# Attention units of a hybrid diffusion trunk put into a fixed TensorE order

## The chip, the cores and the metric

The kernel runs on one core of one Trainium2 chip. The metric is the device time of one execution in microseconds (us). Everything is float32; matmuls marked fp32r take operands that were split into a high part and a remainder, so most products are three matmuls.

## The reference, cut to what matters

One layer of a trunk: 512 latent and 128 context tokens (640 together), width 1024. One input projection feeds four mixers; each mixer's output goes through a branch matrix to width 1024, is multiplied by a sigmoid gate of its own, and the four are summed; an output projection and an MLP follow. Three of the mixers are attention with 8 heads: windowed (`sq`, `sk`, `sv`, with a sink logit), grouped-query (`gq`, ...) and multi-head latent attention (`mla_*`).

```python
def _joint_attention(q, segments, scale, sink=None):
    ...
        s = jnp.einsum(spec, q, k).astype(jnp.float32) * scale
    ...
    m = jnp.max(s, axis=-1, keepdims=True)
    e = jnp.exp(s - m)
    den = jnp.sum(e, axis=-1, keepdims=True)
    p = e / den
    ...
        o = jnp.einsum(spec, p[..., off:off + n_k].astype(v.dtype), v)
```

A latent query block of 128 tokens reads 640 keys (context and latent); in the windowed mixer it reads 384 or 512. The context query block reads 128 keys.

## The kernel before, in words

Activations lie transposed in SBUF as `hT` (channels on partitions, 640 tokens). The attention work is cut into **units**: a unit (`unit`, L800) is one query block `qt` (0 to 3 latent, 4 context) of a pair of heads. It does the scores on TensorE into PSUM, the negated row maximum on DVE (L818 or L835), the exponential with row sums on ACT (L819 or L840), the reciprocal on DVE (L821 or L847), the multiplication of the 128 x W weights `P` by it on POOL (L809), the transposes of `P` by TensorE (L856) with copies to `PT` on ACT and DVE (L858, L860), the products with the values (L1009 in the windowed and grouped-query mixers, L1185 in MLA), and the evacuation as a split pair (L506, L142).

- Where W is 640, the two heads are done one after the other: each has a PSUM tile `sc` of its own, two banks with 320 columns used in each. Two such tiles exist (pool `pss`, four banks). Otherwise both heads share one `sc` tile, a bank for each.
- `run_gqa` runs 20 units (two groups `j2` of 10) for the windowed mixer (n=1) and again for the grouped-query mixer (n=3). The queries of the second group are projected between the groups. Then `gates(n)` projects that branch's gates: 8 column groups (`gate_steps`), each of two halves of 24 matmuls of 320 columns (L365 to L367, into `mm`), a copy to `sig` by ACT (L694), and a sigmoid over 128 x 2560 after four groups (L697).
- `merge(n, ...)` multiplies a mixer's projected output by its gates (L365 to L367 with `oh`, `ol`, then L980, L981).
- `mla` projects queries and keys from low-rank latents. For each head pair `jj` it makes Q (`mQ`), rotary queries (transposes into `pj`, L1152), values (L1166) and keys (`mK`, `Kp`), and then five units; here a score is three matmuls (L949, L950, L1182). Beside them `side` holds 27 steps (L211 and what follows) of the next modulation rows, eight matmuls and a 512 KB load each, three steps after each unit. `ada_ps` is one bank of which two halves are used in turn.

Weights come by DMA on the queue of SyncE (`wr`, three buffers), are copied to `wh` by POOL (L139) and get their remainder `wl` from DVE (L142).

The order of instructions on each engine is made by the framework's scheduler when the program is built, from the program order and the dependencies; a block under `in_order(PE)` keeps the traced order on TensorE. Before the change, the attention stages are not under it. All 128-wide PSUM tiles come from eight banks: `sc` 4, `mm` 2 (in MLA `ada_ps` and `pj` instead), `tp`/`pv` 2.

Of the kernel before, what the change touches and what calls it, by code (L numbers as in the profile page):

```python
# [20 lines left out]
T = TS + TP  # L21
# [43 lines left out]
def trunk(ctx, tc, I, O):  # L65
# [26 lines left out]
    pss = ctx.enter_context(tc.tile_pool(name="pss", bufs=2, space=PSUM))  # L92
# [15 lines left out]
    def sc_tile():  # L108
        return pss.tile([128, 2, 512], F32, tag="sc", name="sc")
# [387 lines left out]


# [189 lines left out]
    def gate_steps(n, sig):  # L688
# [16 lines left out]
    with tc.tile_pool(name="hx", bufs=1) as hx:  # L705
# [25 lines left out]
        fill, due = dense(), 0.0  # L731

        def beside(share):

            nonlocal due
            due += share
            while due > 0:
                due -= next(fill, 100.0)

        with in_order(PE):  # L740
            for hp in range(2):
                lev = hgrn_levels(*qfk[hp], hx)
                while True:
                    try:
                        beside(next(lev))
                    except StopIteration as e:
                        A, QP = e.value
                        break
                for share in hgrn_out(hp, *qfk[hp], A, QP, hx):
                    beside(share)  # L750
            for _ in fill:
                pass
# [47 lines left out]
    def unit(n, c, heads, qt, nk, score, pv_mm, sink=False, bands=None):  # L800
# [11 lines left out]
        if W > 512:  # L812

            for i in range(2):
                sv = sc_tile()[:, :, 0:W // 2]
                for a in range(2):
                    score(sv[:, a], i, a * (W // 2), W // 2)
                V.tensor_reduce(out=negm[:, i:i + 1], in_=sv, axis=AX.XY, op=ALU.max, negate=True)  # L818
                S.activation(out=Pt[:, i, 0:W].rearrange("p (a n) -> p a n", a=2), in_=sv, func=AF.Exp,  # L819
                             bias=negm[:, i:i + 1], accum_out=den[:, i:i + 1])  # L820
                V.reciprocal(out=rden[:, i:i + 1], in_=den[:, i:i + 1])  # L821
                weigh(i)
        else:
            sv = sc_tile()[:, :, 0:W]
# [26 lines left out]
        for j, kt in enumerate(range(0, nk, 2)):  # L851
            kn = min(2, nk - kt)
            tp = tp_tile().rearrange("p (k i) t -> p k i t", i=2)
            for i in range(2):
                for kk in range(kn):
                    PE.transpose(out=tp[:, kk, i], in_=Pt[:, i, 128 * (kt + kk):128 * (kt + kk) + 128], identity=ident)  # L856
            if j % 2 == 0:
                S.activation(out=PT[:, kt:kt + kn], in_=tp[:, 0:kn], func=AF.Copy)  # L858
            else:
                V.tensor_copy(out=PT[:, kt:kt + kn], in_=tp[:, 0:kn])  # L860
        o = pv_tile()
        for kt in range(nk):
            for a in range(2):
                pv_mm(o[64 * a:64 * a + 64, 0:128], a, kt, PT[:, kt, a], kt == 0, kt == nk - 1)
        o_evac(n, c, 128 * qt, o[:, 0:128])

    def gqa_like(n, qn, kn, ck, cv, ok, ov_, norm):
# [38 lines left out]
        def queries(j2):  # L906
            QQ = big(F32R, 2, 2, T, name="Q")
            Q = [QQ[:, a] for a in range(2)]
            wq = wgroup(q_cols(OFF[qn], j2), 0, 256)
            bank = mm_tile if j2 else sc_bank  # L910
            ps = tok_block(wq, 256, hT, 0, bank())
            for tt in range(NT):
                x = prepare(tt, ps, 4, norm and norm[0], None)
                if tt + 1 < NT:
                    ps = tok_block(wq, 256, hT, tt + 1, bank())

                tp = (mp_tile if j2 else tp_tile)()
                for j in range(2):
                    PE.transpose(out=tp[:, j], in_=x[:, 128 * j:128 * j + 128], identity=ident)
                q_split(tp[:, 0:2], [x[:, :, 128 * tt:128 * tt + 128] for x in Q], 0.125)  # L920
            return Q
        return queries, K, Vt
# [67 lines left out]
    def run_gqa(n, queries, Q0, K, Vt, tiles, sink, bands):  # L990
        for j2 in range(2):
            Q = queries(j2) if j2 else Q0
            for qt, i in [(qt, i) for qt in range(5) for i in range(2)]:
                ks, j = tiles(qt), 2 * j2 + i

                def score(out, a, k0, kn):
                    Qa = Q[a][:, i, 128 * qt:128 * qt + 128]
                    done = 0
                    while done < kn:
                        first = ks[(k0 + done) // 128] * 128 + (k0 + done) % 128  # L1000
                        step = 128 - (k0 + done) % 128
                        while done + step < kn and ks[(k0 + done + step) // 128] * 128 == first + step:
                            step += 128
                        step = min(step, kn - done)
                        qk_mm(out[:, done:done + step], Qa, K_part(K, first, step), a)
                        done += step

                def pv_mm(out, a, kt, PTa, start, stop):
                    PE.matmul(out=out, lhsT=Vt[:, ks[kt], 64 * a:64 * a + 64], rhs=PTa, start=start, stop=stop)  # L1009
                unit(n, j, (j, 4 + j), qt, len(ks), score, pv_mm, sink=sink, bands=bands(qt))  # L1010

    queries, K, Vt = gqa_like(1, 'sq', 'sk', I['cache_swa_k'][0, 0], I['cache_swa_v'][0, 0], O['swa_k'], O['swa_v'], None)
# [4 lines left out]
    run_gqa(1, queries, Q0, K, Vt, swa_tiles, True, swa_bands)  # L1017
    sig = gates(1)
# [5 lines left out]
    queries, K, Vt = gqa_like(3, 'gq', 'gk', I['cache_gqa_k'][0, 0], I['cache_gqa_v'][0, 0], O['gqa_k'], O['gqa_v'],  # L1024
# [4 lines left out]
    run_gqa(3, queries, Q0, K, Vt, full_tiles, False, lambda qt: None)  # L1029
    sig3 = gates(3)  # L1030


    def mla():
# [96 lines left out]
        psm[1].close()  # L1130
        ex = ExitStack()
        psx = ex.enter_context(tc.tile_pool(name="psx", bufs=1, space=PSUM))
        ada_ps = psx.tile([128, 2, 256], F32, name="ada_ps")
        side.extend(ada_part(2, ada_ps[:, 0], modrow) + ada_part(3, ada_ps[:, 1]) + ada_part(4, ada_ps[:, 0]))

        def pj_tile():
            return psx.tile([128, 512], F32, tag="pj", name="pj")
# [3 lines left out]
        for jj in range(4):  # L1141
# [5 lines left out]
            t_block(wu['uq'][0], 128 * jj, cX, ev, bank=sc_bank)  # L1147
            for t4, tts in ((0, range(4)), (4, range(4, 5))):
                tp = pj_tile().rearrange("p (i t) -> p i t", t=128)
# [3 lines left out]
                for a in range(2):  # L1153
# [6 lines left out]
                    copy_r(to[64:128], f(to[0:64]))  # L1160
            if jj % 2 == 0:
                wv = [(x[0][:, 128 * jj:128 * jj + 256], x[1][:, 128 * jj:128 * jj + 256]) for x in wu['ukv'][1]]
                for kt in range(6):
                    ps = tok_block(wv, 256, kX, kt, pj_tile())
                    for i in range(2):
                        S.activation(out=Vs[jj + i][:, kt], in_=ps[:, 128 * i:128 * i + 128], func=AF.Copy)  # L1166
            Vt = Vs[jj]
            K = new_K("mK")

            def ev(ps, t0, tn):  # L1170
                for a, b in ((t0, min(t0 + tn, T)), (max(t0, T), t0 + tn)):
                    if a < b:
                        k_evac(ps[:, a - t0:b - t0], K, a, b - a)
            t_block(wu['ukv'][0], 128 * jj, kX, ev, halves=((0, 384), (384, 384)), bank=sc_bank)
            for qt in range(5):
                ks = full_tiles(qt)

                def score(out, a, k0, kn):
                    t = slice(128 * qt, 128 * qt + 128)
                    b = slice(ks[0] * 128 + k0, ks[0] * 128 + k0 + kn)  # L1180
                    qk_mm(out, Qa[a][:, t], K_part(K, b.start, kn), a, last=False)
                    PE.matmul(out=out, lhsT=QR[a][:, t], rhs=KRo[:, b], start=False, stop=True)  # L1182

                def pv_mm(out, a, kt, PTa, start, stop):
                    PE.matmul(out=out, lhsT=Vt[:, ks[kt], 64 * a:64 * a + 64], rhs=PTa, start=start, stop=stop)  # L1185
                unit(n, jj, (0, 1), qt, len(ks), score, pv_mm)
                side_steps(3)
# [155 lines left out]
```

## Time and profile before

| | us |
|---|---|
| median of 3 runs | 1501.13 (1498.35 to 1501.28) |
| profiled execution | 1502.2 |
| its span, first to last instruction | 1500.4 |
| mean granted TensorE clock | 0.991 of full |

The profiled execution is 1.1 us above the median, and 1.8 us lie around its span. In the timeline a row gives start and length in us, engine, line, operation, output and inputs; a matmul's length includes its way through the array, so the distance between two starts is what one costs when they follow each other. The stages are: windowed units 327 to 475, keys and queries of the grouped-query mixer and a merge 475 to 575, grouped-query units to 690, MLA's projections with a merge and gates to 795, MLA's head preparation and units to 945, the last merge to 975.

### The profile page before, as it was taken

How to read it: one execution, taken by the hardware profiler on the slowest of the kernel's cores; microseconds unless marked ns; L12 is line 12 of the kernel's file. 1: busy time of each engine (PE TensorE's matmuls, PEld its weight loads, DVE VectorE, ACT ScalarE, POOL GpSimd, SP SyncE). 2: the span in 40 equal slices, each digit the busy share in tenths (PEclk: the TensorE clock that was granted, in tenths of full speed). 3: DMA queues.
4: the chain of work that ended last, by engine and by line, in shares of the span. 5: the costliest groups of instructions: out<-in, count | busy, mean ns of one | idle time of the engine just before them, and what ended most of it. 6: DMA issues, size and time to landing. Idle time of an engine off the chain costs nothing.

```text
span 1500.4 us, 26709 instructions
## 1 busy us (share of the span) xinstructions
PE 1430.5 (95%) x10969; PEld 1302.2 (87%) x10969; DVE 796.1 (53%) x1447; ACT 481.4 (32%) x1161; POOL 432.2 (29%) x456
## 2 busy tenths in 40 slices
PE   6999999899999999999998998998999999999996
PEld 5898998899898998999996677988898998898995
DVE  4347657476643788433725566746243444444446
ACT  4334333333443235442124565225220110110112
POOL 2015325243321545222213334124111111112114
PEclk9999999999999999999999999999999999999998
DMA  9421212121112131112224601221343223222221
GB/s 328 128 85 58 70 49 64 50 68 50 45 43 59 34 84 37 33 42 74 80 68 143 224 15 43 99 85 56 112 129 101 80 71 98 71 70 71 75 66 70
DMA packets 138225, 121.17 MB, mean 81 GB/s; under 512 B 22296, under 2 KB 119412, under 8 KB 138104
## 3 DMA queue, kind: packets, MB, share of 16 engines
q1 hardware_dynamic: 138104, 119.47, 26.4%
q8 instruction: 86, 1.41, 0.4%
q14 instruction: 35, 0.29, 0.1%
HBM read 115.96 MB, written 3.49 MB: 80 GB/s over the span
## 4 chain that ended last, share of the span: by engine, by line
PE 70%; issue 13%; DVE 8%; POOL 5%; ACT 2%; DMA 1%; POOLq 0%; DVEq 0%; SPq 0%; ACTq 0%
PE mm L365 12%; PE mm L366 11%; PE mm L367 11%; PE mm L381 4%; PE mm L382 4%; PE mm L383 4%; PE tp L856 3%; POOL wh L139 3%; PE pv L1009 3%; PE sc L383 3%; PE sc L381 2%; PE sc L382 2%; PE sc L949 2%; PE sc L950 2%; DVE wl L142 1%
## 5 line engine op out<-in xcount | busy, mean ns | idle before, releaser
L139 POOL TENSOR_SCALAR wh<-wr 128x1024 fp32r<-128x1024 f32 (+3 forms) x136 | 156.7, 1154 | 536.4 <-PE mm L366 290.4
L142 DVE TENSOR_TENSOR wl<-wr,wh 128x1024 fp32r<-128x1024 f32 (+3 forms) x160 | 198.9, 1247 | 160.0 <-POOL wh L139 120.8
L365 PE MATMUL mm<-hTh,wh 128*128 128x320 f32 x704 | 220.5, 313 | 2.0 <-DVE qA L520 0.9
L367 PE MATMUL mm<-hTh,wl 128*128 128x320 f32 x704 | 219.2, 311 | 0.0
L366 PE MATMUL mm<-hTl,wh 128*128 128x320 f32 x704 | 218.2, 310 | 0.0
L366 PE MATMUL mm<-h2Tl,wh 128*128 128x320 f32 x512 | 159.4, 311 | 1.1 <-DVE h2Tl L142 1.1
L365 PE MATMUL mm<-h2Th,wh 128*128 128x320 f32 x512 | 159.5, 312 | 0.0
L367 PE MATMUL mm<-h2Th,wl 128*128 128x320 f32 x512 | 159.2, 311 | 0.0
L809 POOL TENSOR_SCALAR P<-P,rden 128x640 f32<-128x640 f32 (+3 forms) x120 | 84.5, 713 | 184.0 <-DVE rden L821 80.7
L365 PEld LDWEIGHTS mm<-hTh,wh 128*128 128x128 f32 x704 | 132.2, 188 | 3.9 <-DVE qA L520 1.0
L367 PEld LDWEIGHTS mm<-hTh,wl 128*128 128x128 f32 x704 | 132.2, 188 | 0.9 <-issue 0.7
L366 PEld LDWEIGHTS mm<-hTl,wh 128*128 128x128 f32 x704 | 132.2, 188 | 0.5 <-issue 0.3
L382 PE MATMUL mm<-wl,hidh 128*128 128x512 f32 x320 | 124.8, 390 | 0.6 <-DVE wl L142 0.6
L381 PE MATMUL mm<-wh,hidh 128*128 128x512 f32 x320 | 125.3, 392 | 0.0
L383 PE MATMUL mm<-wh,hidl 128*128 128x512 f32 x320 | 124.6, 389 | 0.0
L1292 ACT ACTIVATE relu<-mm 128x320 f32<-128x320 f32 x64 | 28.0, 438 | 281.1 <-PE mm L367 281.1
L366 PEld LDWEIGHTS mm<-h2Tl,wh 128*128 128x128 f32 x512 | 97.1, 190 | 1.7 <-DVE h2Tl L142 1.5
L365 PEld LDWEIGHTS mm<-h2Th,wh 128*128 128x128 f32 x512 | 96.9, 189 | 0.7 <-issue 0.4
L367 PEld LDWEIGHTS mm<-h2Th,wl 128*128 128x128 f32 x512 | 97.0, 189 | 0.0
L1293 DVE TENSOR_TENSOR relu<-relu 128x320 f32<-128x320 f32 x64 | 40.4, 632 | 100.8 <-ACT relu L1292 100.8
L1305 DVE TENSOR_TENSOR y<-mm,y 128x512 f32<-128x512 f32 x70 | 48.2, 689 | 81.9 <-PE mm L383 81.9
L381 PE MATMUL sc<-wh,hTh 128*128 128x256 f32 (+2 forms) x224 | 72.0, 322 | 5.5 <-DVE tx L935 2.4
(355 smaller groups left out, 3238.4 us busy)
## 6 DMA issues: line engine op xcount, KB each, us to landing
wr<-in_w_in SPq DMA_DIRECT2D x56, 512.0 KB, 3.7
wada<-in_w_ada SPq DMA_DIRECT2D x48, 512.0 KB, 4.5
wr<-in_w_mlp_in SPq DMA_DIRECT2D x32, 512.0 KB, 4.0
wr<-in_w_mlp_out SPq DMA_DIRECT2D x32, 512.0 KB, 3.6
wr<-in_w_in SPq DMA_DIRECT2D x64, 64.0 KB, 2.1
wr<-in_w_branch SPq DMA_DIRECT2D x8, 512.0 KB, 4.1
wr<-in_w_branch SPq DMA_DIRECT2D x16, 256.0 KB, 4.1
wr<-in_w_out SPq DMA_DIRECT2D x8, 512.0 KB, 3.6
```

The costliest lines, as they stand in the source:

```text
L139: G.tensor_scalar(out=out, in0=src, scalar1=1.0, scalar2=1.0, op0=ALU.mult, op1=ALU.mult)
L142: V.tensor_tensor(out=out, in0=src, in1=f(hi), op=ALU.subtract)
L365: PE.matmul(out=ps[:, 0:tn], lhsT=wh, rhs=a, start=(k == 0), stop=False)
L366: PE.matmul(out=ps[:, 0:tn], lhsT=wh, rhs=b, start=False, stop=False)
L367: PE.matmul(out=ps[:, 0:tn], lhsT=wl, rhs=a, start=False, stop=(k == nk - 1))
L381: PE.matmul(out=ps[:, 0:n], lhsT=a, rhs=w[k][0], start=(start and k == 0), stop=False)
L382: PE.matmul(out=ps[:, 0:n], lhsT=a, rhs=w[k][1], start=False, stop=False)
L383: PE.matmul(out=ps[:, 0:n], lhsT=b, rhs=w[k][0], start=False, stop=(stop and k == nk - 1))
L809: G.tensor_scalar(out=Pt[:, i, 0:W], in0=Pt[:, i, 0:W], scalar1=rden[:, i:i + 1], scalar2=1.0, op0=ALU.mult, op1=ALU.mult)
L856: PE.transpose(out=tp[:, kk, i], in_=Pt[:, i, 128 * (kt + kk):128 * (kt + kk) + 128], identity=ident)
L1009: PE.matmul(out=out, lhsT=Vt[:, ks[kt], 64 * a:64 * a + 64], rhs=PTa, start=start, stop=stop)
L1305: V.tensor_tensor(out=ys, in0=ps, in1=ys, op=ALU.add)
```

## The change

Each attention stage is written as a pipeline under `in_order(PE)` (`run_units`): for every new unit TensorE gets the scores of both heads, the first part of the transposes of the unit before, some other dense work, the rest of these transposes, the products of the unit two before, and again dense work. `Fill` hands out the dense work by shares.

- In `run_gqa` the dense work is the second group's queries and the gates; the sigmoids come after the stage (`apart=True`). The two `sig` tiles are allocated ahead of the units.
- In `mla` the preparation of the next head pair is the dense work (`heads`); that of the first runs ahead, values included. The side steps are two after each unit's products.
- In `mla` the scores of both heads lie in one tile `scores` of three banks, used by all units: columns 0 to 639 and 640 to 1279, cut at 512 and 1024, so that a head's 640 columns are 512 and 128, or 384 and 256. `pj` gets two buffers. For this, `pss` is closed and opened with `psm`.

```diff
-    psm = [None, None]
+    psm = [None, None, None]
...
+        psm[2] = psm[1].enter_context(tc.tile_pool(name="pss", bufs=2, space=PSUM))
...
+    class Fill:
+        def __init__(self, steps):
+            self.steps, self.due = steps, 0.0
+        def give(self, share):
+            self.due += share
+            while self.due > 0:
+                self.due -= next(self.steps, 1e9)
+        def rest(self):
+            for _ in self.steps:
+                pass
...
-            if kk % 4 == 3:
+            if kk % 4 == 3 and not apart:
                 S.activation(out=g, in_=g, func=AF.Sigmoid)
...
-        if W > 512:
-
-            for i in range(2):
-                sv = sc_tile()[:, :, 0:W // 2]
+        def wide(i):
+            if banks is None:
+                sv, to = sc_tile()[:, :, 0:W // 2], Pt[:, i, 0:W].rearrange("p (a n) -> p a n", a=2)
                 for a in range(2):
                     score(sv[:, a], i, a * (W // 2), W // 2)
...
+            else:
+                sv, to = banks[:, W * i:W * i + W], Pt[:, i, 0:W]
+                k0 = 0
+                while k0 < W:
+                    kn = min(W - k0, 512 - (W * i + k0) % 512)
+                    score(sv[:, k0:k0 + kn], i, k0, kn)
+                    k0 += kn
+            V.tensor_reduce(out=negm[:, i:i + 1], in_=sv, axis=AX.X if banks is not None else AX.XY, op=ALU.max, negate=True)
+            S.activation(out=to, in_=sv, func=AF.Exp, bias=negm[:, i:i + 1], accum_out=den[:, i:i + 1])
+            V.reciprocal(out=rden[:, i:i + 1], in_=den[:, i:i + 1])
+            weigh(i)
...
+        def turn(part):
+            for j, kt in list(enumerate(range(0, nk, 2)))[2 * part:2 * part + 2]:
...
+        if W > 512:
+            return lambda: wide(0), lambda: wide(1), turn, products
+        return both, lambda: None, turn, products
+
+    def run_units(units, beside, after=lambda: None):
+        cur = old = None
+        units = iter(units)
+        with in_order(PE):
+            while True:
+                new = next(units, None)
+                if new is None and cur is None and old is None:
+                    break
+                if new:
+                    new[0]()
+                    new[1]()
+                if cur:
+                    cur[2](0)
+                beside()
+                if cur:
+                    cur[2](1)
+                if old:
+                    old[3]()
+                    after()
+                beside()
+                old, cur = cur, new
...
+        def dense():
+            gate = gate_steps(n, sig, True)
+            for i, share in enumerate(second):
+                yield share
+                if i % 2 == 0:
+                    yield next(gate)
+            yield from gate
...
+        fill = Fill(dense())
+        run_units(units(), lambda: fill.give(0.5))
+        fill.rest()
+        for g in sig:
+            S.activation(out=g, in_=g, func=AF.Sigmoid)
...
+        scores = psx.tile([128, 3, 512], F32, name="scores").rearrange("p a n -> p (a n)")
...
+        preludes = [None] + [heads(jj, got[jj], lambda: psx.tile([128, 512], F32, tag="pj", name="pj", bufs=2))
+                             for jj in range(1, 4)]
...
+            return unit(n, jj, (0, 1), qt, len(ks), score, pv_mm, banks=scores)
+        run_units(units(), lambda: fill.give(0.4), lambda: side_steps(2))
```

## Rows read from the trace of the kernel before

**Rows 1.** The page, busy time and share of the span by engine

```profile
PE 1430.5 (95%) x10969; PEld 1302.2 (87%) x10969; DVE 796.1 (53%) x1447; ACT 481.4 (32%) x1161; POOL 432.2 (29%) x456
```

**Rows 2.** Windows by stage: busy us and count by engine, clock, DMA share, GB/s

```profile
327.00:475.00 148.00, 146.86 (x1124) 133.55 (x1122) 84.47 (x203) 60.20 (x171) 42.72 (x58) 1.00 0.22 54
...
575.00:690.00 115.00, 112.25 (x926) 105.60 (x927) 53.35 (x111) 53.21 (x130) 34.59 (x43) 1.00 0.16 44
690.00:795.00 105.00, 105.00 (x694) 104.53 (x693) 45.20 (x97) 17.59 (x56) 24.59 (x31) 1.00 0.28 77
795.00:820.00 25.00, 20.97 (x150) 14.29 (x148) 15.89 (x35) 14.34 (x30) 12.37 (x19) 0.86 0.50 159
820.00:945.00 125.00, 113.32 (x1002) 90.07 (x998) 75.99 (x166) 71.10 (x199) 47.17 (x71) 1.00 0.29 94
```

**Rows 3.** Groups by line and shape, 795 to 945 us: busy, mean ns, idle before

```profile
L856 PE MATMUL tp<-ident,P 128*128 128x128 f32 x168 | 26.5, 278 | 1.1 <-DVE modcol L242 1.1
...
L949 PE MATMUL sc<-mK,mQ 128*128 128x320 f32 x64 | 23.2, 363 | 2.1 <-DVE Kp L142 1.3 <-ACT P L819 0.5
```

**Rows 4.** Timeline 818.6 to 821.3 us: an MLA head's way from scores to weights

```profile
818.80 0.31 PE L1182 MATMUL sc<-ckv,mQ 128*128 128x320 f32 x1
...
818.95 0.60 PE L856 MATMUL tp<-ident,P 128*128 128x128 f32 x4
819.15 0.82 DVE L818 TENSOR_REDUCE negm<-sc 128x1 f32<-128x640 f32 x1
...
820.01 0.79 ACT L819 ACTIVATE P<-sc,negm 128x640 f32<-128x640 f32 x1 [0.78 <-DVE negm L818]
...
820.92 0.16 DVE L821 RECIPROCAL rden<-den 128x1 f32<-128x1 f32 x1 [0.95 <-ACT P L819]
821.00 0.31 PE L1182 MATMUL sc<-ckv,mQ 128*128 128x320 f32 x1
821.15 0.31 PE L949 MATMUL sc<-mK,mQ 128*128 128x320 f32 x1
821.18 0.80 POOL L809 TENSOR_SCALAR P<-P,rden 128x640 f32<-128x640 f32 x1 [1.20 <-DVE rden L821]
```

**Rows 5.** Timeline 835.5 to 840 us: the two halves of the bank `ada_ps`

```profile
835.81 0.64 PE L211 MATMUL ada_ps<-wada,cpad 128*32 128x256 f32 x8
...
836.52 0.39 ACT L228 ACTIVATE mrow<-ada_ps 128x256 f32<-128x256 f32 x1 [0.31 <-PE ada_ps L211]
...
839.44 0.64 PE L211 MATMUL ada_ps<-wada,cpad 128*32 128x256 f32 x8
```

**Rows 6.** The page, DMA issues: count, KB each, us to landing

```profile
wada<-in_w_ada SPq DMA_DIRECT2D x48, 512.0 KB, 4.5
```

**Rows 7.** Timelines at 981 and 903 us: matmuls of 512 columns, products of a unit

```profile
980.73 0.39 PE L382 MATMUL sc<-wl,yXh 128*128 128x512 f32 x1
980.96 0.39 PE L383 MATMUL sc<-wh,yXl 128*128 128x512 f32 x1
...
903.04 1.31 PE L1185 MATMUL pv<-PT,mVt 128*64 128x128 f32 x20 [0.72 <-ACT PT L858]
```

**Rows 8.** Groups by line and shape, 395 to 470 us, windowed units

```profile
L139 POOL TENSOR_SCALAR wh<-wr 128x1024 fp32r<-128x1024 f32 x7 | 7.3, 1044 | 13.1 <-PE mm L366 13.1
L809 POOL TENSOR_SCALAR P<-P,rden 128x512 f32<-128x512 f32 x8 | 5.4, 693 | 14.6 <-DVE rden L847 14.6
L840 ACT ACTIVATE P<-sc,negm 128x512 f32<-128x512 f32 x8 | 5.4, 683 | 4.8 <-PE tp L856 4.8
L835 DVE TENSOR_REDUCE negm<-sc 128x2 f32<-128x1024 f32 x4 | 4.9, 1225 | 0.1
...
L831 DVE TENSOR_TENSOR sc<-sc,win_sb 128x512 f32<-128x512 f32 x4 | 2.8, 698 | 1.4 <-PE sc L950 1.4
...
L697 ACT ACTIVATE sig<-sig 128x2560 f32<-128x2560 f32 x1 | 2.3, 2339 | 0.0
```

**Rows 9.** Windows after a stretch in which TensorE stood still

```profile
497.00:503.00 6.00, 4.09 (x20) 4.09 (x21) 4.36 (x11) 0.69 (x3) 3.46 (x5) 0.72 0.60 147
808.00:818.00 10.00, 8.78 (x52) 5.08 (x53) 4.63 (x10) 4.27 (x9) 3.99 (x8) 0.66 0.79 264
```

More of the change, by code (lines that the diff above doesn't have):

```diff
@@ L749, in trunk @@
                 for share in hgrn_out(hp, *qfk[hp], A, QP, hx):
[L750 to L752 removed]
+                    fill.give(share)
+            fill.rest()
         wtile.act = False
@@ L986, in merge @@
                 t_block(wb, 128 * m, OT[n], ev)
[L990 to L1010, printed above, removed]
@@ L1012, in trunk, with run_gqa, units, one @@
-    queries, K, Vt = gqa_like(1, 'sq', 'sk', I['cache_swa_k'][0, 0], I['cache_swa_v'][0, 0], O['swa_k'], O['swa_v'], None)
+    def run_gqa(n, query_steps, Q0, K, Vt, tiles, sink, bands):
+        Q1, sig = [], [big(F32, 4, T, name="sig") for _ in range(2)]
+        second = query_steps(1, Q1)
+        def dense():
[5 more added lines that the diff above has]
+            yield from gate
+        def units():
+            for j2 in range(2):
+                for qt, i in [(qt, i) for qt in range(5) for i in range(2)]:
+                    if j2:
+                        for _ in second:
+                            pass
+                    yield one(Q1 if j2 else Q0, j2, qt, i)
+        def one(Q, j2, qt, i):
+            ks, j = tiles(qt), 2 * j2 + i
+            def score(out, a, k0, kn):
+                Qa = Q[a][:, i, 128 * qt:128 * qt + 128]
+                done = 0
+                while done < kn:
+                    first = ks[(k0 + done) // 128] * 128 + (k0 + done) % 128
+                    step = 128 - (k0 + done) % 128
+                    while done + step < kn and ks[(k0 + done + step) // 128] * 128 == first + step:
+                        step += 128
+                    step = min(step, kn - done)
+                    qk_mm(out[:, done:done + step], Qa, K_part(K, first, step), a)
+                    done += step
+            def pv_mm(out, a, kt, PTa, start, stop):
+                PE.matmul(out=out, lhsT=Vt[:, ks[kt], 64 * a:64 * a + 64], rhs=PTa, start=start, stop=stop)
+            return unit(n, j, (j, 4 + j), qt, len(ks), score, pv_mm, sink=sink, bands=bands(qt))
+        fill = Fill(dense())
+        run_units(units(), lambda: fill.give(0.5))
+        fill.rest()
+        for g in sig:
+            S.activation(out=g, in_=g, func=AF.Sigmoid)
+        return sig
@@ L1174, in mla @@
[L1174 to L1187, printed above, removed]
+                    yield 0.25
@@ new lines, in heads @@
+            got += [Qa, QR, K]
+        got = [[] for _ in range(4)]
+        banks = [sc_bank, mm_tile]
+        for _ in heads(0, got[0], lambda: banks.reverse() or banks[0]()):
+            pass
+        psm[1].close()
+        ex = ExitStack()
+        psx = ex.enter_context(tc.tile_pool(name="psx", bufs=1, space=PSUM))
+        scores = psx.tile([128, 3, 512], F32, name="scores").rearrange("p a n -> p (a n)")
+        ada_ps = psx.tile([128, 2, 256], F32, name="ada_ps")
+        side.extend(ada_part(2, ada_ps[:, 0], modrow) + ada_part(3, ada_ps[:, 1]) + ada_part(4, ada_ps[:, 0]))
```

121 lines of the change are left out of this document (63 added, 58 removed).

## The prediction

> **What bounds the kernel now.** I read the page first: TensorE has a matmul in flight for 95% of the span, DVE for 53%, ACT and POOL for about 30% [rows 1]. So time can only come out of TensorE's own gaps, and I went to the windows by stage for them [rows 2]. In the windowed units (327 to 475 us) TensorE is busy 146.86 of 148 us, in the grouped-query units (575 to 690) 112.25 of 115, in the stretch to 795 that has merges and gates 105.00 of 105. The scheduler already lays gate work between the units there; what is left to win is 1.1 and 2.8 us. MLA is different: 4.0 us idle in its start (795 to 820), 11.7 us in 820 to 945. Then I read the groups by shape and the timeline inside MLA, to price a unit and the way from scores to weights [rows 3, 4].
>
> TensorE is therefore the bound in all these stages, and a new wait of TensorE costs its full length, since the fixed order leaves it nothing else to take.
>
> **The change part by part.** *MLA, both heads in three banks.* This part decides. Head 0 has columns 0 to 639 of `scores`, head 1 columns 640 to 1279; a bank ends at 512 and 1024. So the bank in the middle holds the last 128 columns of head 0 and the first 384 of head 1. The traced order is: scores of head 0, its maximum (DVE), its exponential (ACT), both reading that bank, and then scores of head 1, which begin by writing it. In the kernel before, each head had two banks for itself. If engines are kept apart by banks, the first matmul of head 1 waits for head 0's exponential, and `in_order(PE)` puts everything behind it: the transposes of the unit before, dense work, products, side steps.
>
> No row of before shows this wait or its absence outright. The nearest is `ada_ps`, whose halves are one bank: after the last matmul of one half (835.81), ACT copies it out at 836.52 for 0.39 us, and the other half is first written at 839.44 [rows 5]. That fits a wait by bank, but also a scheduler that had other work. Bounds: below, nothing. Above, the chain of an undisturbed head: its last score matmul starts at 818.80, the maximum at 819.15, the exponential at 820.01 and ends at 820.80, so 2.00 us [rows 4]; the next engine to use the result starts 0.12 later; a 128-column matmul itself takes about 0.11 (four transposes in 0.60, one of them lasting 0.28 [rows 3, 4]). That is 2.0 us each time. With the exponential behind another 0.8 us ACT instruction it would be 2.8. There are 4 head pairs of 4 latent units, 16 such places (3 x 64 score matmuls of 320 columns, 12 to a unit [rows 3]): 0, **32** or 45 us. I take 32, because without the wait TensorE would write the middle bank while DVE or ACT reads it, in every unit, and in the one shared bank of before nothing of the kind is seen.
>
> The Trainium skill (PSUM — Partial Sum Buffer, section PSUM bank collisions raise a hardware error) says that two engines must not touch the same bank in the same 32 partitions at once, whatever the columns, and that PSUM is to be guarded by bank and not by address. By that rule the wait is there in all 16 units, and this rule speaks against the change; by the row on `ada_ps` alone it could be nothing, and the sum below would be 32 us lower.
>
> *The cut at 512.* Head 0 has a 512 and a 128 where it had two of 320: 0.23 [rows 7] and 0.11 for twice 0.15 [rows 4], 0.04 more for each of three operand pairs; head 1's 384 and 256 come out even. 16 x 3 x 0.04: **+2 us**.
>
> *MLA, the fixed order and the spread of preparation and side steps.* Here the idle time goes that comes where a head pair's keys and queries are made right before their use. At most all 11.7 us of 820 to 945 [rows 2], at least nothing; the fixed order can add waits of its own (part two of the transposes needs a buffer that ACT is still emptying), but with 2 us standing in each unit most of these chains are done in time. I take **-11.7**. A unit's products are 20 matmuls in 1.31 us and its ten transposes about 1.1, so with scores of 1.9, the wait and two side steps of 0.64 [rows 4, 5, 7] a unit lasts over 7 us; a side step's load lands 4.5 us after issue [rows 6], with three buffers and SP's queue free but for these, so the loads stay hidden: 0, and some 8 us (0.5 for each of 16 units) if they came late. The start (795 to 820) keeps its length: the first pair's values move ahead of its scores, but DVE and ACT are busy 15.9 and 14.3 of these 25 us with the same keys and queries.
>
> The Trainium skill (Perfetto Trace Analysis, section Identifying the Most-Contended Engine) says that matmul busy time is a poor measure of distance to the peak, since matmuls are pipelined, and prefers the busy share of the weight loads. The trace agrees as far as it goes: the full stretch 690 to 795 has 105.00 and 104.53 us, while 820 to 945 has 113.32 against 90.07 [rows 2]. By this rule 34.9 us and not 11.7 could go; that is a rival below.
>
> *Windowed and grouped-query units.* Removed at most 1.1 + 2.8 = 3.9 us of idle time. Against it stands the windowed chain with W = 512: 0.35 to the mask, 0.70, maximum 1.23, exponentials 2 x 0.68, weights 2 x 0.69 on POOL [rows 8], four small DVE steps of 0.16 with hand-overs [rows 4], together 5.7 us. TensorE has from one unit's scores to its transposes a gate half (24 x 0.15 = 3.5), 8 transposes (0.9), products (0.9) and the next scores (4 x 0.23 = 0.9), 6.2 us. It fits, by 0.5; where POOL's weight copy of 1.04 us stands in front, every second unit, it is about 0.5 late: 8 such units, at most 3 to 4 us. Together **-1** (from -4 to +6). The grouped-query chain has one head's maximum and exponential at a time and far more room.
>
> *Sigmoids.* Both (2.34 us each [rows 8]) now run behind the last gate instead of one in the middle. After the windowed stage ACT is wanted by the next keys, so up to 2.3 us can show; I take **+1**. In the grouped-query stage merges and gates cover it. The exchange of ACT's tables that goes with the early sigmoid falls away; ACT is not the bound, so 0.
>
> *Merge and gate rows after MLA.* The `mm` banks come free only after the last exponential, so what ran beside the last units runs behind them, while the transposes and products still drain: 0, up to 3.
>
> Sum: 32 + 2 - 11.7 - 1 + 1 = +22.3 on the profiled execution's 1502.2 us, so 1524.5; that execution stands 1.1 above the median of the runs, which gives **1523 us**. Its own range is 1512 (three quarters of the places wait) to 1537.
>
> **The rivals.** *No wait in the middle bank*: dependencies go by columns, or the copy is quick enough. Then 1523 - 32 = 1491, faster. The place is head 1's first score matmul; it decides from about 1.4 us per unit downward (22.3 / 16). For it: the pools hand out regions, and nothing in before stalls by a bank. Against: `ada_ps`. 18 in 100.
>
> *The fixed order removes the short gaps too*: the 34.9 us by weight loads instead of 11.7 [rows 2], so 1523 - 23 = 1500, no change to speak of. For it: 820 to 945 has weight loads in only 72% of its time. Against: part of that is transposes and products, whose loads are short by nature. 12 in 100.
>
> *The clock*: after TensorE stood still, 497 to 503 and 808 to 818 show a mean grant of 0.72 and 0.66 [rows 9], that is, the lower level of 1.2 GHz for part of them, at a loss of 1.7 and 3.4 us of full-speed work. If the new stalls bring 1.7 us at every second of 16 places: +14, 1537. Against: 820 to 945 has a grant of 1.00 with many gaps. 8 in 100.
>
> **How the numbers follow.** Forecast 58, no wait 18, short gaps 12, clock 8, anything else 4. A change of under 0.2% (3 us) cannot be told from none here. Faster: 18 + 3 of the short gaps + 2 = 23; same: 6; slower: 58 + 3 + 8 + 2 = 71. The range for 8 in 10 reaches from the case without the wait to that of the clock, 1489 to 1538.
>
> **What would show it.** Right: in MLA a TensorE gap of about 2 us between head 0's and head 1's scores in each latent unit, released by ACT's exponential (L819's successor); windowed and grouped-query stages within a few us of 148 and 115; MLA's last products some 20 us later. Wrong: head 1's scores follow at once, or the gap is filled; a windowed stage with gaps before the transposes; a grant below 1 all through MLA.

## The result, and the profile after

The changed kernel takes 1593.26 us (median of 4 runs, 1592.86 to 1598.44) against 1501.2 (1498.35 to 1504.35): ratio 1.0621, 95% interval 1.059 to 1.0651. Forecast were 1523, and 1489 to 1538; the direction was right, the size was not: +92 us for +22. The profiled execution has a span of 1591.4 us at a mean grant of 0.972 (before: 1500.4 at 0.991).

The page of the changed kernel, busy time by engine, answers to [rows 1]:

```profile
PE 1459.2 (92%) x10969; PEld 1329.9 (84%) x10969; DVE 792.4 (50%) x1447; ACT 480.1 (30%) x1161; POOL 429.4 (27%) x456
```

The same 10969 matmuls. The span grew by 91.0 us in two parts: TensorE stands idle 1591.4 - 1459.2 = 132.2 us where it was 69.9, that is +62.3; and it is busy 28.7 us longer with the same work.

The windows of the changed kernel by stage, columns as in [rows 2]:

```profile
300.00:514.40 214.40, 194.30 (x1489) 180.95 (x1487) 110.57 (x274) 76.15 (x216) 63.41 (x85) 0.98 0.19 47
514.40:580.00 65.60, 63.40 (x452) 61.68 (x453) 51.23 (x116) 13.93 (x34) 25.38 (x27) 0.97 0.29 66
580.00:722.00 142.00, 124.89 (x1037) 114.25 (x1037) 62.17 (x133) 60.14 (x155) 41.51 (x52) 0.99 0.13 34
722.00:832.20 110.20, 110.20 (x723) 109.14 (x722) 46.85 (x101) 21.93 (x62) 24.58 (x32) 1.00 0.29 75
832.20:860.00 27.80, 18.70 (x92) 15.64 (x91) 17.47 (x36) 17.17 (x42) 12.82 (x20) 0.82 0.07 20
860.00:1028.00 168.00, 128.39 (x1002) 102.61 (x1002) 70.61 (x156) 67.27 (x184) 46.32 (x70) 0.86 0.27 88
```

The bounds are those of the work (the first merge behind the windowed units, the last gate of branch 2, MLA's last products), so the like stretches of before are these:

```profile
300.00:498.90 198.90, 192.97 (x1494) 178.16 (x1492) 112.84 (x275) 77.79 (x216) 63.80 (x85) 1.00 0.20 50
498.90:575.00 76.10, 75.19 (x588) 72.44 (x588) 63.20 (x143) 25.39 (x63) 34.28 (x36) 0.98 0.24 57
690.00:795.30 105.30, 105.30 (x696) 104.83 (x695) 45.20 (x97) 17.59 (x57) 24.70 (x32) 1.00 0.28 76
```

With the row for 575 to 690 in [rows 2]: idle time of TensorE grew from 5.9 to 20.1 us in the windowed stage, from 3.7 to 19.3 from there to the gates of branch 2, and in MLA (its start included) from 15.7 to 48.7. The sum is +62.8, all of the growth in idle time. The rest of the loss is busy time, and most of it lies from MLA on: MLA is busy 147.1 us with 1094 matmuls, where before had 134.0 with 1150, and the stretch behind it, which got the other 56, 546.2 for 538.2. Together that is 21 us more with the same 4159 matmuls. MLA's longer row has a grant of 0.86 where [rows 2] have 1.00. (That both these rows count 1002 matmuls is chance; they are not the same ones: 192 of side steps for 132, and none of the 48 of a merge.)

MLA's idle time has one main source. The waits by group, changed kernel, 860 to 1028 us (waited for: us, times, longest):

```profile
PE scores L1001 <- ACT P L832: 32.5, 15, 3.1
PE tp L872 <- ACT PT L874: 2.1, 7, 0.3
```

A sixteenth place lies just ahead of this window, at 853.64 (1.89 us), which makes 34.4 us. The timeline shows one of these places, head 0's last score, its maximum and exponential, and head 1's first score:

```profile
880.94 0.28 PE L1276 MATMUL scores<-ckv,mQ 128*128 128x128 f32 x1
881.25 0.82 DVE L831 TENSOR_REDUCE negm<-scores 128x1 f32<-128x640 f32 x1 [1.57 <-PE scores L1276]
882.17 0.79 ACT L832 ACTIVATE P<-scores,negm 128x640 f32<-128x640 f32 x1 [2.81 <-DVE negm L831]
...
883.11 0.44 PE L1001 MATMUL scores<-mK,mQ 128*128 128x384 f32 x1 [1.89 <-ACT P L832]
```

Nothing runs on TensorE from 881.22 to 883.11: this is the wait that was forecast, 2.15 us a place for 2.0. The grouped-query stage shows what was not forecast: all of its 17.1 us are waits for copies of transposes (waits by group, 580 to 722, then the timeline of one unit):

```profile
PE tp L872 <- DVE PT L876: 5.8, 6, 1.9
PE pv L1080 <- ACT PT L874: 5.1, 6, 2.5
PE tp L872 <- ACT PT L874: 4.9, 8, 0.9
PE pv L1080 <- DVE PT L876: 1.3, 3, 0.5
```

```profile
674.61 1.03 PE L872 MATMUL tp<-ident,P 128*128 128x128 f32 x8
674.96 1.21 DVE L142 TENSOR_TENSOR wl<-wr,wh 128x1024 fp32r<-128x1024 f32 x1
675.14 0.79 ACT L832 ACTIVATE P<-sc,negm 128x640 f32<-128x640 f32 x1 [1.07 <-DVE negm L831]
...
675.92 0.59 ACT L874 ACTIVATE PT<-tp 128x512 f32<-128x512 f32 x1
676.09 0.81 DVE L831 TENSOR_REDUCE negm<-sc 128x1 f32<-128x640 f32 x1
...
676.56 0.44 PE L872 MATMUL tp<-ident,P 128*128 128x128 f32 x2 [0.92 <-ACT PT L874]
676.83 0.68 DVE L876 COPY PT<-tp 128x512 f32<-128x512 f32 x1
677.04 0.38 ACT L874 ACTIVATE PT<-tp 128x256 f32<-128x256 f32 x1 [0.53 <-PE tp L872]
...
677.48 1.31 PE L1080 MATMUL pv<-PT,Vt 128*64 128x128 f32 x20 [0.47 <-ACT PT L874]
```

Part two of the transposes follows part one at once and waits 0.92 us for a buffer, since ACT copies only behind its exponential and DVE only behind a maximum and a weight remainder (`wl`, 1.21 us); the products then wait 0.47 for the last copy. The 24 dense matmuls come behind the products, as they do in nearly every unit of the two stages.

### The profile page after: what moved, and what is told of

It is laid out like the page before. It is cut to its first block, busy times and chain, and to the rows that moved or that the text cites. A ratio compares the mean times of both kernels' runs of the same rounds, so it can differ in the third digit from the quotient of the medians.

```text
span 1591.4 us, 26694 instructions
## 1 busy us (share of the span) xinstructions
PE 1459.2 (92%) x10969; PEld 1329.9 (84%) x10969; DVE 792.4 (50%) x1447; ACT 480.1 (30%) x1161; POOL 429.4 (27%) x456
## 4 chain that ended last, share of the span: by engine, by line
PE 64%; issue 13%; DVE 11%; ACT 6%; POOL 5%; DMA 1%; SPq 0%; POOLq 0%; DVEq 0%; ACTq 0%
PE mm L365 11%; PE mm L366 10%; PE mm L367 10%; PE mm L381 4%; PE mm L382 4%; PE mm L383 3%; POOL wh L139 3%; PE sc L383 2%; PE sc L381 2%; PE sc L382 2%; PE pv L1080 2%; PE tp L872 2%; DVE negm L831 2%; DVE wl L142 2%; ACT P L832 1%
## 5 line engine op out<-in xcount | busy, mean ns | idle before, releaser
L142 DVE TENSOR_TENSOR wl<-wr,wh 128x1024 fp32r<-128x1024 f32 (+3 forms) x160 | 195.1, 1223 | 148.2 <-POOL wh L139 109.3
L365 PE MATMUL mm<-hTh,wh 128*128 128x320 f32 x704 | 223.9, 318 | 2.0 <-DVE qA L534 0.9
L872 PE MATMUL tp<-ident,P 128*128 128x128 f32 x456 | 77.1, 303 | 20.0 <-ACT PT L874 7.2
L1387 DVE TENSOR_TENSOR relu<-relu 128x320 f32<-128x320 f32 x64 | 40.4, 632 | 101.4 <-ACT relu L1386 101.3
```

What stands on the lines that cost most here:

```text
L142: V.tensor_tensor(out=out, in0=src, in1=f(hi), op=ALU.subtract)
L365: PE.matmul(out=ps[:, 0:tn], lhsT=wh, rhs=a, start=(k == 0), stop=False)
L1387: V.tensor_tensor(out=sq, in0=sq, in1=sq, op=ALU.mult)
```

## The experiments

Each run has a run of the kernel before on the same chip. Those single runs lay between 1499.98 and 1507.12, so differences of less than some 7 us between single runs prove little alone (all rows but the first and the last two are single runs); idle and busy time of TensorE and the grant are those of the page of each run.

| run | us | over before | idle | busy | grant |
|---|---|---|---|---|---|
| changed kernel | 1593.3 | +92.1 | 132.2 | 1459.2 | 0.972 |
| e1 MLA undone | 1539.2 | +39.2 | 98.4 | 1439.0 | 0.986 |
| e2 other stages undone | 1556.4 | +56.4 | 101.3 | 1453.3 | 0.971 |
| e3 scores first | 1560.5 | +60.6 | 115.2 | 1443.2 | 0.981 |
| e4 fill first | 1574.6 | +74.6 | 115.6 | 1456.9 | 0.966 |
| e5 both | 1537.9 | +35.8 | 94.0 | 1442.1 | 0.977 |
| e6 free order | 1534.7 | +32.5 | 87.1 | 1445.8 | 0.978 |
| e7 preparation spread | 1533.8 | +31.6 | 93.5 | 1438.5 | 0.982 |
| e8 one unit later | 1545.0 | +42.9 | 98.9 | 1444.3 | 0.976 |
| e9 four banks | 1578.3 | +71.2 | 126.7 | 1449.8 | 0.972 |
| e10 one `pj` | 1624.4 | +117.3 | 150.3 | 1472.3 | 0.957 |
| e11 free, four banks | 1511.0 | +3.9 | 72.4 | 1436.8 | 0.984 |
| e12 free, scores first | 1516.5 | +9.3 | 74.2 | 1440.4 | 0.983 |
| e13 no remainder | 1563.6 | +60.6 | 109.8 | 1451.7 | 0.972 |
| e14 free, earlier | 1511.2 | +8.2 | 70.6 | 1438.8 | 0.985 |
| e15 free, score banks | 1504.0 | +1.0 | 70.1 | 1432.1 | 0.988 |
| e16 sigmoids inside | 1598.3 | +95.4 | 131.4 | 1465.2 | 0.965 |
| e17 first pair free | 1496.1 | -5.5 | 65.3 | 1430.3 | 0.987 |
| e18 sigmoids behind | 1494.7 | -6.9 | 65.4 | 1430.3 | 0.988 |

**Which stage.** In e1 MLA has the code of before, in e2 `run_gqa` has (`for u in units(): u[0](), u[1](), u[2](0), u[2](1), u[3]()` and then `gates(n)`, no fixed order).

> The changed kernel with MLA as before (each head's scores in two banks of its own, no fixed order, preparation of a head pair right before its units, three side steps); the windowed and grouped-query stages keep the change. The trace of the changed kernel puts about 49 us of the 92 in MLA (its last products come 86 us later, gates of branch 2 already 37 later). Theory (the stages' costs add up, 49 of them MLA's): 1540 to 1550 us. Rival (MLA pays only for what comes late from the stages ahead, or the half clock has another cause): above 1565 us.

> The changed kernel with the windowed and grouped-query stages as before (no fixed order, the second group's queries between the groups, gates and their sigmoids by the scheduler); MLA keeps the change. Theory (these two stages cost 37 us by the milestones: 15.5 to the start of the first merge behind the windowed units, 37 to the end of branch 2's gates): 1553 to 1560 us. Rival (they only cover each other's idle time, and MLA would lose more with them undone): above 1575 us.

What e1 keeps, the other two stages, costs 39.2; what e2 keeps, MLA, costs 56.4. They make 95.6 for the 92.1 of the whole: the costs add up, and over a third does not lie in MLA. The rivals of both fall (e1 is 0.8 us below its range, e2 inside).

**The bank, or the order.** e3 has both heads' scores ahead of both maxima:

```diff
                     k0 += kn
+                yield
             V.tensor_reduce(out=negm[:, i:i + 1], in_=sv, ...)
...
+        def heads_first():
+            w = [wide(0), wide(1)]
+            for _ in range(2):
+                for x in w:
+                    next(x, None)
         if W > 512:
+            if banks is not None:
+                return heads_first, lambda: None, turn, products
```

> The changed kernel, but in MLA the scores of both heads are traced ahead of both maxima and exponentials; the same three banks, the same fixed order. Bank theory: the 15 gaps of about 2.5 us at head 1's first score matmul go, 38 us in the trace, and with them part of the half clock in MLA: 1540 to 1558 us. Rival (the time belongs to the fixed order, or to transposes waiting for weights, and only moves to the next wait): 1575 us or more.

33 us less, 17 of them idle time and 16 busy time, at a better grant. The 32.5 us of waiting turned partly into other waits; its row for 833 to 995 us is `PE scores L1009 <- ACT P L833` with 10.8 us at 6 places, where a unit's scores wait for the unit before, and preparation steps wait 3.7, 2.5 and 1.9. e9 keeps the traced order and gives each head two banks again, paid for by one `pj` buffer less; e10 is the control with only the buffer less.

```diff
-        scores = psx.tile([128, 3, 512], F32, name="scores").rearrange("p a n -> p (a n)")
+        psm[2] = ex.enter_context(tc.tile_pool(name="pss", bufs=2, space=PSUM))
...
-... tag="pj", name="pj", bufs=2)
+... tag="pj", name="pj", bufs=1)
```

> The changed kernel, but in MLA each head's scores get two banks of their own again, 320 columns in each, with the traced order unchanged (head 0's maximum and exponential ahead of head 1's scores); the bank is taken from pj, which has one buffer. Bank theory: the wait at head 1's scores goes without any change of order, 33 us as with scores first, less what the single pj buffer costs: 1552 to 1575 us. Rival (it was the place of the maximum in the order, not the bank): the 2.5 us gaps stay, 1593 us or more.

> Control for the run with four banks: the changed kernel with its three banks of scores, but one pj buffer. Theory: with the preparation in the fixed order each step waits for the one buffer, some 30 steps of up to 1 us, 1600 to 1620 us, and the run with four banks is 30 to 40 us below this one. Rival (the second buffer is worth nothing): within 3 us of the changed kernel.

Waits by group in MLA from 860 us on, first of e10, then of e9:

```profile
PE scores L1001 <- ACT P L832: 31.1, 15, 3.0
PE pj L365 <- DVE mK L142: 7.7, 3, 3.0
```

```profile
PE pj L365 <- DVE mK L142: 8.9, 3, 3.5
PE pj L365 <- DVE mQ L784: 6.3, 3, 2.1
PE tp L872 <- ACT PT L874: 5.5, 11, 1.2
```

With banks of its own for each head the wait is gone with no change of order, and the time falls by 46 us against the control. So it is the sharing. But in e9 each head has a tile of its own too, and other rows tell bank from tile. A context unit writes its scores to columns 0 to 255, all in the first bank; head 1's exponential of the unit before reads columns 640 to 1279, in the other two. In e6, which has the three banks in a free order (below), TensorE waits for it all the same (timeline: head 0's exponential, head 1's, the context unit's first score):

```profile
956.02 0.79 ACT L832 ACTIVATE P<-scores,negm 128x640 f32<-128x640 f32 x1
...
959.86 0.79 ACT L832 ACTIVATE P<-scores,negm 128x640 f32<-128x640 f32 x1 [1.65 <-DVE negm L831]
960.55 0.19 ACT L832 ACTIVATION_READ_ACCUMULATOR P<-scores,negm 128x1 f32 x1
...
960.80 0.33 PE L1001 MATMUL scores<-Kp,mQ 128*128 128x128 f32 x1 [1.40 <-ACT P L832]
```

Nothing reads the first bank after 956.8, yet the first score starts at 960.80. In the twelve runs that have the shared tile, none of 228 units begins its scores before head 1's exponential of the unit before has ended; the earliest begins 0.14 us behind it. So the program waits by the whole tile of three banks. That explains the 34.4 us too; that the bank in the middle costs anything by itself is not shown. The Trainium skill (PSUM — Partial Sum Buffer, section PSUM bank collisions raise a hardware error) asks for a guard by bank and not by address. The wait at head 1's first score fits that, since head 0 has columns of the same bank; the waits in the first bank go beyond it. e9 came out 3 us above its range, since one buffer costs more than I allowed: e10 is 4 us above its own.

**The place of the dense work.** e4 hands out the share in one piece ahead of part two of the transposes, e5 has e3's edit too.

```diff
-        run_units(units(), lambda: fill.give(0.5))
+        shares = cycle((1.0, 0.0))
+        run_units(units(), lambda: fill.give(next(shares)))
```

> The changed kernel, but in the windowed and grouped-query stages each unit's whole share of dense work stands between the two parts of the transposes, none behind the products (shares 1.0 and 0 in place of 0.5 and 0.5). Theory (in the second group the share always fell behind the products, so part two of the transposes and the products wait for copies with nothing between): 20 to 35 us less than the changed kernel, 1558 to 1573 us. Rival (the fixed order costs it wherever the dense work stands, the wait being for weights from POOL): 1583 us or more.

> Both single edits of the changed kernel together: in MLA both heads' scores ahead of both maxima, in the other two stages the whole dense share between the two parts of the transposes. They act in different stages, so they should add up: 33 + 19 us below the changed kernel, 1536 to 1546 us. Rival (one sets free what the other then waits for): above 1552 us.

e4 takes 18.7 us off (1.6 us short of its range), and the grouped-query stage is nearly whole again:

```profile
575.00:716.00 141.00, 139.38 (x1156) 130.85 (x1154) 68.82 (x149) 67.65 (x168) 46.01 (x56) 1.00 0.14 38
```

1.6 us idle of 141, where the changed kernel had 17.1 of 142. e5 is where the sum of e3 and e4 puts it. What e4 leaves is mostly in the windowed stage, which stands idle 16.1 us (300 to 513.7); its largest wait there, and the start of such a unit in its timeline:

```profile
PE tp L873 <- POOL P L816: 11.2, 12, 3.0
```

```profile
429.59 1.23 DVE L143 TENSOR_TENSOR wl<-wr,wh 128x1024 fp32r<-128x1024 f32 x1 [2.31 <-POOL wh L140]
...
429.95 0.34 PE L1003 MATMUL sc<-K,Q 128*128 128x384 f32 x1
...
431.06 0.42 DVE L848 TENSOR_TENSOR sc<-sc,win_sb 128x256 f32<-128x256 f32 x1
431.51 0.96 DVE L849 TENSOR_REDUCE negm<-sc 128x2 f32<-128x768 f32 x1
```

The scores are there at 430.29, the mask starts at 431.06: DVE takes a weight remainder first. e13 leaves these remainders of the gates out (the matmul takes the high part in their place, so the gates lose precision: a probe, not a kernel to keep); e8 gives the weights a second unit of time.

```diff
+        if wtile.bare:            # set for gates of the two mixers
+            return v(hi), v(hi)
         rest(lo[:, 0:m], raw[:, 0:m], hi[:, 0:m])
```

> The run with the dense share first, but the gate weights of the windowed and grouped-query mixers get no remainder: DVE's subtraction of 1.23 us per weight group is left out, and TensorE takes the high part in its place, so it has the same number of matmuls (the gates lose some precision). Theory (in the windowed units this subtraction stands on DVE in front of the mask and the maximum at the start of every gate unit, and is what makes the weights late for the transposes): the 16 us of waiting transposes fall to 6 or less, 8 to 14 us below the run with the dense share first. Rival (the chain of mask, maximum, exponentials and POOL's weights is too long by itself): within 4 us of it.

```diff
-                old, cur = cur, new
+                old, cur, mid = cur, mid, new
```

> Scores first and dense share first, and all transposes and products one unit later (transposes of the unit two before, products of the one three before), so that the weights have two units of time. Theory (in the windowed units 16 us go on transposes waiting for weights, whose chain is longer than one unit): 12 to 20 us below the run with both edits. Rival (with two P tiles the next exponential now waits for the transposes, which moves the wait to the scores): no gain or a loss of up to 15 us.

e13 takes 11 us off e4, 5.8 of them idle time (3.3 in the windowed stage); the wait for POOL's weights falls from 11.2 to 6.1 us (10 places). So the remainder makes about half of this wait, and the chain is too long by itself for the other half: neither theory alone. (The 16 us of the expectations are all idle time of the stage, of which this wait is 11.2.) In e8 that wait is gone, but scores wait for exponentials (16.3 us at 11 places in MLA, 3.2 us in the grouped-query stage): 7 us worse than e5, the rival.

**The fixed order itself.** e6 drops `in_order(PE)` from `run_units`; e7 is e5 with the preparation in MLA given by 0.3 at a time.

> The changed kernel without the fixed TensorE order in its attention stages: the same program order, the same three banks, the scheduler free to reorder. Theory (the waits cost their full length because the fixed order leaves TensorE nothing else; the scheduler would fill them): 1505 to 1545 us, and the gap ahead of head 1's scores filled. Rival (the layout itself, three banks, two pj buffers, early sig tiles, sets the waits): 1575 us or more.

> Scores first and dense share first as in the run before, and in MLA the next head pair's preparation handed out by 0.3 in place of 0.4 at a time, so that two preparation steps seldom follow each other directly. Theory (with two pj buffers the second or third step in a row waits for ACT and DVE to empty one, seen as 3.8, 2.0 and 1.8 us in front of preparation matmuls): 6 to 10 us below the run with both edits. Rival (the emptying is late wherever the step stands): within 2 us of it.

With the order free the wait at head 1's first score is 1.2 us at 2 places for 34.4 at 16, and idle time falls from 132 to 87: the scheduler fills nearly all of that wait, and much of the other stages' new idle time. In its place 9.9 us at 9 places stand at the first score of the next unit, where the same tile is waited for. e7 gains 4.1 us on e5, less than the 6 expected and within what single runs scatter.

**Where the gain of 11.7 us is.** e11, e12, e14, e15, e17 and e18 have the other stages undone and MLA's units only traced as a pipeline, with no fixed order. e11: four banks, one `pj`, preparation by 0.3; e12: three banks with scores first, two `pj`, by 0.3; e14: e11 by 0.5; e15: e14 with score banks for the preparation; e17: e15 with the first pair prepared behind the exchange of pools; e18: e17 with both sigmoids behind the last gate.

```diff
+        turns = cycle((sc_bank, lambda: psx.tile([128, 512], F32, tag="pj", name="pj", bufs=1)))   # e15
+        for _ in heads(0, got[0], lambda: next(turns)()):                                          # e17
+            pass
```

> Windowed and grouped-query stages as before; MLA as a pipeline in the traced order only (no fixed TensorE order), two banks for each head as before, one pj buffer, preparation traced between the units by 0.3. Theory (the fixed order and the shared bank are all that costs; the spread preparation is worth up to some us): 1492 to 1506 us. Rival (the traced pipeline itself, transposes a unit later and two side steps, costs): 1515 us or more.

> As the run before it, but with the three shared banks and both heads' scores ahead of both maxima, two pj buffers. Theory (scores first undoes the whole cost of the shared bank): within 5 us of that run. Rival (the three banks also hold up the next unit's scores, since a unit's tile is free only when both heads' exponentials are done): 10 to 25 us above it.

> The free order with four banks of scores, with the preparation of the next head pair traced by 0.5 at a time in place of 0.3, so that it is done earlier. Theory (there the last pair's queries came late behind the merge's weight remainders on DVE, gaps of 3.7 and 2.5 us, and a stretch at the half clock): 5 to 9 us below that run, some us below the kernel before. Rival (the single pj buffer makes it late in any case): within 2 us of it.

> As the run before it, but the preparation takes pj and a bank of the score tiles in turn, as the kernel before does, in place of pj alone. Theory (the one pj buffer is what holds the preparation): 2 to 6 us below the run before it. Rival (the score tiles are the scarcer, so the scores wait): 3 to 10 us above it.

> As the run with free order and score banks for the preparation, but the first head pair is prepared after the pools have been exchanged, with the same banks in turn as the later pairs. Theory (in that run 5 us of TensorE gaps stand at the start of MLA, where the first pair's steps follow each other through two banks, and they are no longer the order's fault but this place's): 3 to 6 us below it, 1497 to 1501 us, up to 0.3% below the kernel before. Rival (keys and queries of the first pair take DVE and ACT as long whatever the banks): 1502 to 1506 us, no different from the kernel before.

> As the run before it, with both sigmoids of a stage behind its last gate, the one part of the change in the other two stages that has paid so far. Theory (with the sigmoids inside, the changed kernel took 5 us more; in the free order the 2.3 us on ACT also delay an exponential in each stage): 1 to 4 us below the run before it. Rival (the scheduler already places the sigmoid where ACT is free): within 1 us of it, or 1 to 2 us above, when the merge waits for the last one.

e11 is back near the kernel before (1507.1 on that chip), 5 us above its range: the pipeline alone wins nothing. e12 is 5.5 above e11, just over what its theory allows, so three banks with scores first cost little in the free order. The start time of the preparation is not why (e14 equals e11). e15 points to the one buffer, but does not show it: it is 7.2 us below e14, no more than single runs scatter, and that is busy time (1432.1 for 1438.8), while idle time stays (70.1 for 70.6). Of e17, 6 runs give 1496.06 (1493.94 to 1497.41), ratio 0.996 [0.9946, 0.9974], of e18 1494.68, 0.995 [0.9934, 0.9965], against 11 runs of before: both lie half a per cent or less below the kernel before, with 1 outside their intervals, and do not differ from each other. (e17 is 0.9 below its range.) The windows of e17 for MLA's start and units:

```profile
795.30:820.00 24.70, 21.59 (x151) 14.96 (x149) 16.11 (x34) 15.75 (x36) 11.92 (x19) 0.86 0.44 144
...
820.00:945.00 125.00, 117.01 (x1026) 95.77 (x1027) 79.91 (x176) 70.15 (x196) 48.12 (x72) 0.97 0.32 107
```

8.0 us idle and 1026 matmuls where [rows 2] have 11.7 and 1002.

**The sigmoids.**

> The changed kernel with the sigmoids back inside the stages, each behind its four gates. Theory of the prediction (+1 us for the two at the end, at most 2.3): 0 to 2 us less than the changed kernel. Rival (inside the pipeline the 2.3 us on ACT and the exchange of tables delay exponentials that TensorE waits for): 2 to 8 us more.

5 us more than the changed kernel, all of it in busy time (1465.2 for 1459.2 at a lower grant), none in idle time. The sign is against my +1; the size is no more than single runs scatter.

## Why the prediction was wrong, step by step

- *Wait in the middle bank, +32*: right in place and size (34.4 us at 16 places; e9 against e10 shows that sharing is the cause), so the rival without a wait falls. The reason given, engines kept apart by banks, is not what the runs show: the wait goes by the tile (e3, e6). Both reasons give the same price at this place, so the number stands; what follows from it for the next unit's scores (10.8 us in e3) does not come from the bank.
- *Windowed and grouped-query units, -1 (-4 to +6)*: this is the first step that failed. Measured are +14.2 and +15.6 us of idle time. I compared the length of the chain with TensorE's work in a whole unit, and did not follow where `give` puts the work: a gate half counts 1.0, so two shares of 0.5 release one step, and in nearly every unit it comes behind the products. So nothing stood between the two parts of the transposes, where a copy is waited for (e4: -18.7). I had named this wait for a buffer in MLA and left it out here, and gave the grouped-query chain "far more room"; its 17.1 us are all such waits. And in the windowed sum I put POOL's weight copy ahead of the chain but not DVE's remainder of 1.23 us (e13: the wait for weights 11.2 to 6.1 us).
- *The clock, a rival at 8 in 100 and +14*: the second step that failed. It came with the forecast and not in its place, and the sum had busy time at nothing. Over the span it grew by 28.7 us with the same 10969 matmuls; MLA's grant fell to 0.86. Part of this may be matmuls that no longer overlap with one ahead, which the rows do not part from the clock. A stall on the path had to be priced with what it does to the work behind it.
- *MLA's idle time, -11.7*: the third, the upper bound taken as the value. Idle time other than that wait is 48.7 - 34.4 = 14.3 us against 15.7: 1.4 was won. In the fixed order preparation steps wait for their buffers instead (e3, e10); in the free order 4.6 are won (795.3 to 945: 15.7 to 11.1 in e17, with 27 more matmuls).
- *The short gaps too* (34.9 us): falls. The Trainium skill (Perfetto Trace Analysis, section Identifying the Most-Contended Engine) measures the room by the weight loads. e17 got 95.77 us of them into 820 to 945 where [rows 2] have 90.07: some of that room exists, and no order tried here used more of it.
- *Cut at 512* (+2) was not tried by itself. *Sigmoids* (+1): against the sign of e16, too small to settle. *Rows after MLA* (0 to 3): from MLA's end to the end of the span 563.4 us for 555.4, over the bound; 56 more matmuls have moved there, and idle time is the same (17.2 us), so it is work and not a wait. The signs named for being wrong came: gaps before the transposes in the windowed stage, a grant below 1 all through MLA, and MLA's last products 86 us later for some 20. One slip in the sums: with three quarters of the places waiting it is 1515, not 1512.

So the span's +91.0 is 33 us of idle time in MLA (34.4 of the wait for the shared tile, less 1.4), 30 in the other two stages, and 28.7 of slower or less overlapped matmuls. The direction was no luck: the wait that decides the forecast is there, at its price. The 69 us above the forecast are, to within 2 us, the three steps that failed (31, 28.7 and 10.3). Left open is how the 28.7 divide.

## What to carry to other kernels

Fixing TensorE's order turned hand-overs behind it into full-length waits here (1593 us for 1535 without), so before doing it follow one unit step by step and ask of each pair of neighbours what the second needs, and which other instructions that producer's queue holds first; a sum over the unit hides this. Two heads packed into one PSUM tile are tied together: here the next writer waited for the last reader of the whole tile, also in a bank that this reader does not touch. Write everything into the tile first (e3), or spend the banks for a tile each (e9). The same pipeline with the scheduler free to reorder stood at +32 us in place of +92; what did pay, a little (0.4 to 0.5%), was MLA alone in traced order, with banks of its own for each head, banks in turn for the preparation, and the first pair prepared behind the exchange of pools.

## What the runs showed of the hardware that was not expected

TensorE's own work grew with its waits. In MLA all eight windows of 25 us from 825 to 1025 have a grant between 0.72 and 0.93 in the changed kernel, where [rows 2] have 1.00 with 11.7 us of idle time; e3, which took away the 2.2 us waits, has 0.93 over 860 to 995. A 128-column transpose averaged 346 ns for 278 [rows 3], the same 168 in both:

```profile
L872 PE MATMUL tp<-ident,P 128*128 128x128 f32 x168 | 33.5, 346 | 2.1 <-ACT PT L874 2.1
```

And an engine's queue can hold up another through a load that neither needs. Timeline of e3, where TensorE waits 4.92 us for head 1's exponential before a unit's first score, in the first bank:

```profile
962.53 0.19 ACT L833 ACTIVATION_READ_ACCUMULATOR P<-scores,negm 128x1 f32 x1
...
963.36 1.04 POOL L139 TENSOR_SCALAR wh<-wr 128x1024 fp32r<-128x1024 f32 x1 [3.61 <-DMA wr<-in_w_branch]
964.43 1.23 DVE L142 TENSOR_TENSOR wl<-wr,wh 128x1024 fp32r<-128x1024 f32 x1 [2.69 <-POOL wh L139]
...
965.58 0.15 DVE L834 RECIPROCAL rden<-den 128x1 f32<-128x1 f32 x1
965.65 0.81 DVE L832 TENSOR_REDUCE negm<-scores 128x1 f32<-128x640 f32 x1
...
967.43 0.79 PE L1009 MATMUL scores<-mK,mQ 128*128 128x512 f32 x1 [4.92 <-ACT P L833]
```

DVE's reciprocal could go at 962.72, when ACT's row sums are there, and head 1's maximum earlier; both stand behind a remainder for the next merge, whose weight lands so late that POOL's copy starts at 963.36.
